# Delta rule's inverse: which engine splits the weights of the blocks beside it, and in which order the blocks run

## The chip, the cores and the metric

One NeuronCore of a Trainium2 chip runs the whole program. TensorE multiplies; VectorE, ScalarE and GpSimd do the rest; SyncE's queue (SP) issues nearly all DMAs. The metric is the device time of one execution in microseconds; the median of several runs counts. The granted TensorE clock has two levels here, 1.2 and 2.4 GHz, and the profile gives it as a share of full speed (1.00 is 2.4 GHz).

## The reference, cut to what matters

Two transformer blocks on 512 tokens of width 1024, in f32. The change is in the first block, whose first branch is a gated delta rule over 8 heads and two directions:

```python
a_kk = jnp.where(strict, jnp.einsum('bhnic,bhnjc->bhnij', kb, kc) * gam, 0.0)
sol = lax.linalg.triangular_solve(a_kk + eye, rhs, left_side=True, lower=True, unit_diagonal=True)
...                                     # a scan over the chunks makes o_a from sol
z = proj[..., C_ZA:C_AF].reshape(b, s, GDN_HEADS, GDN_HEAD_DIM)
o_a = _rmsnorm(o_a, norm_a[l]) * jax.nn.silu(z)
gate_a = jax.nn.sigmoid(proj[..., C_GA:C_GB])
gate_b = jax.nn.sigmoid(proj[..., C_GB:IN_COLS])
merged = (gate_a * jnp.einsum('bsc,cd->bsd', o_a, w_branch_a[l])
          + gate_b * jnp.einsum('bsc,cd->bsd', o_b, w_branch_b[l]))
```

Here `proj` is the normed input times `w_in`. The columns for z make 8 blocks of 128, and those for the two gates 16. Neither z nor the gates need the delta rule's result, so they can be worked out while the triangular inverse runs.

## The kernel before, in words

**A projection block.** An f32 product is made of three products of fp32r halves. `wload` (line 74 issues the load of 512 KB into `wraw`) lets ScalarE round the weights to `hi` (line 80) and another engine subtract to get `lo` (line 81), both in one tile `wpair`. `wraw` and `wpair` have three buffers each. `proj` then runs 8 x 3 products of 128 x 512 (lines 96 to 98) into one of the two banks named `pj`. Which engine subtracts is the argument `eng`; without it GpSimd takes the first three of the program and VectorE the others.

**The 24 blocks of this change** come from the generator `gates_z`. Every block ends with ScalarE's tanh out of `pj` into `gth` (line 697) and a store to DRAM (line 700, SP queue): z into `spill_z`, gates into `spill_g`. A z block (j below 8) has one step more: VectorE multiplies with `pj` again (line 699), so its bank of `pj` comes free only after that.

**Where they run.** `Fill` hands out blocks in the generator's order: 14 after the inverse of the 32 x 32 blocks has been issued, 1 inside the merge to 64, 4 inside the merge to 128, 3 in the tail of the delta rule, and 2 at the end of the dilated attention.

**The inverse.** `block_inverse` turns the layout through DRAM (scr), inverts 128 x 2 blocks of 32 x 32 on VectorE in a chain of 30 pairs of a product (line 498) and a sum (line 500), each dependent on the one before it, stores the result (line 503), loads it in another layout (`zd`, `zdT`, line 568) and transposes (lines 509 and 510). `merge32` then needs TensorE for many small products (lines 529, 540, 550), and `gdn_inverse` for those of 64 (lines 595, 604).

**What sets the order.** Each engine works through its own queue in order. The queues' order is made at build time by the framework's planner, which takes the program's order as priority and its own estimates of when an operand is ready; an operation that is ready earlier may be put ahead. A second inverse, in the second transformer block (`rwkv_inverse`, same lines 498 and 500, with `na_proj` and `gates2` beside it), is not touched; its blocks have their `lo` from VectorE.

Of the kernel before, what the change touches and what calls it, by code (L numbers as in the profile page):

```python
# [688 lines left out]
def gates_z(k, act, spill_z, spill_g):  # L689

    nc = k.nc
    for j in range(24):
        w = k.wload(k.a["w_in"][24 + j if j < 8 else 60 + j], eng=nc.gpsimd)
        ps = k.ps("pj")
        k.proj(ps, w, act)
        th = k.fp.tile([P, S], F32, name="gth", bufs=3)
        nc.scalar.activation(th, ps, AF.Tanh, scale=0.5)  # L697
        if j < 8:
            nc.vector.scalar_tensor_tensor(th, th, 1.0, ps, op0=OP.add, op1=OP.mult)  # L699
        nc.sync.dma_start(spill_z[j] if j < 8 else spill_g[j - 8], th)  # L700
        yield True
# [1133 lines left out]
def block1(k, a, pool, dram, tap, new_act, x_mid, x_1, acc_d, stop):  # L1835
# [10 lines left out]
    with pool("gkeep") as k.gk:  # L1846
        with pool("gprep") as k.gp:
            gdn_prep(k, act, R)
        tap("kT", R["kT"])
        fill = Fill(gates_z(k, act, spill_z, spill_g))  # L1850
        with pool("ginv") as k.ip:
            gdn_inverse(k, R, fill)
        tap("zt", R["zt"])
        with pool("gchain") as k.hp:
            gdn_chain(k, R)
        tap("oT", R["oT"])
# [240 lines left out]
```

## Time and profile before

| | |
|---|---|
| median of 3 runs | 2126.0 us (2125.77 to 2127.27) |
| the profiled execution | 2129.85 us, of it span 2128.2 us |
| TensorE products (PE) | 2013.3 us busy, 95% of the span |
| TensorE weight loads (PEld) | 1498.4 us, 70% |
| VectorE (DVE) | 1084.1 us, 51% |
| ScalarE (ACT) | 776.3 us, 36% |
| GpSimd (POOL) | 286.3 us, 13% |

The profile is of one execution, and times inside it are microseconds from the span's start. A busy share is a mean over stages with different limits, so the stage of the change, about 235 to 390 us, is read by itself below. In a timeline an entry in square brackets is the idle time of the engine before the instruction and what ended it; `x2` means two instructions merged into a row.

### The profile page before, as it was taken

Reading aid. Unit: us, or ns where it says so; the run is one execution under the profiler, and the core shown is the slowest. Engines: PE = TensorE matmul, PEld = TensorE weight load, DVE = VectorE, ACT = ScalarE, POOL = GpSimd, SP = SyncE. Lnnn points to the kernel's source line nnn. Section 1 sums busy time; section 2 is a strip of 40 time slices with the busy share of each in tenths; the row PEclk is TensorE's granted clock in tenths of the full one; section 3 lists DMA queues with packets and bytes.
Section 4 is the critical chain, followed back from the end, with each engine's and each line's share of the span. In section 5 each row is a group of like instructions: output and inputs, shape, how many; then the busy total and the mean of one; then the engine's idle time right before and its main releaser. Section 6 shows DMA issues by size and latency. Waiting matters only on the chain.

```text
span 2128.2 us, 30122 instructions
## 1 busy us (share of the span) xinstructions
PE 2013.3 (95%) x12072; PEld 1498.4 (70%) x12072; DVE 1084.1 (51%) x1877; ACT 776.3 (36%) x1357; POOL 286.3 (13%) x261
## 2 busy tenths in 40 slices
PE   6999987999999999999999999989899989799997
PEld 4777776977877787888888876666677778644443
DVE  6887492454234435632333266759337635435555
ACT  4556324432244333442233246645212622211111
POOL 1111342001000002110011001021123001110000
PEclk9999998999999999999999999989899999899999
DMA  4233535844221224422443533682674266499993
GB/s 153 109 129 119 159 135 129 261 147 143 94 73 66 70 80 160 164 91 99 166 142 109 168 108 97 180 231 78 177 249 144 85 227 242 140 421 425 423 423 159
DMA packets 161620, 360.46 MB, mean 169 GB/s; under 512 B 49592, under 2 KB 91192, under 8 KB 147136
## 3 DMA queue, kind: packets, MB, share of 16 engines
q1 hardware_dynamic: 153840, 321.49, 43.2%
q0 software_dynamic: 7200, 35.66, 4.9%
q8 instruction: 96, 1.57, 0.3%
q10 hardware_dynamic: 432, 1.31, 0.2%
q14 instruction: 52, 0.43, 0.1%
HBM read 300.74 MB, written 57.67 MB: 168 GB/s over the span
## 4 chain that ended last, share of the span: by engine, by line
PE 80%; DVE 9%; DMA 4%; issue 3%; POOL 2%; ACT 1%; SPq 1%; DVEq 0%; POOLq 0%; ACTq 0%
PE pj L97 15%; PE pj L98 15%; PE pj L96 15%; PE pj L1648 5%; PE pa L1677 2%; DVE x L500 2%; PE pa L98 2%; PE pa L96 2%; PE pa L97 2%; PE pb L97 1%; PE pb L98 1%; PE pb L96 1%; PE pb L1776 1%; PE pa L1776 1%; DVE xtmp L498 1%
## 5 line engine op out<-in xcount | busy, mean ns | idle before, releaser
L96 PE MATMUL pj<-hh,wpair 128*128 128x512 f32 (+1 forms) x1304 | 524.6, 403 | 8.7 <-DVE gth L699 5.6
L97 PE MATMUL pj<-hl,wpair 128*128 128x512 f32 (+1 forms) x1304 | 523.1, 401 | 1.0 <-DVE hl L151 1.0
L98 PE MATMUL pj<-hh,wpair 128*128 128x512 f32 (+1 forms) x1304 | 523.4, 402 | 0.5 <-issue 0.5
L81 DVE TENSOR_TENSOR wpair<-wraw,wpair 128x1024 fp32r<-128x1024 f32 x200 | 252.9, 1269 | 448.3 <-ACT wpair L80 448.2
L80 ACT CAST wpair<-wraw 128x1024 fp32r<-128x1024 f32 x227 | 236.4, 1046 | 196.1 <-PE pj L98 156.5
L96 PEld LDWEIGHTS pj<-hh,wpair 128*128 128x128 f32 x1304 | 251.9, 193 | 72.4 <-DVE gth L699 6.1
L98 PEld LDWEIGHTS pj<-hh,wpair 128*128 128x128 f32 x1304 | 251.6, 193 | 62.8 <-issue 9.3
L97 PEld LDWEIGHTS pj<-hl,wpair 128*128 128x128 f32 x1304 | 252.2, 193 | 60.3 <-issue 5.7
L1648 PE MATMUL pj<-wtwo,xgT 128*64 128x512 f32 x416 | 96.5, 603 | 0.0
L81 POOL TENSOR_TENSOR wpair<-wraw,wpair 128x1024 fp32r<-128x1024 f32 x27 | 65.8, 2443 | 159.7 <-ACT wpair L80 159.6
L378 DVE SCALAR_TENSOR_TENSOR cacc<-pj,convw,cacc 128x510 f32<-128x510 f32 (+1 forms) x96 | 71.3, 746 | 15.7 <-ACT cacc L374 14.4
L766 ACT COPY d<-pj 128x512 f32<-128x512 f32 x36 | 21.1, 587 | 133.8 <-PE pj L98 133.8
L1648 PEld LDWEIGHTS pj<-wtwo,xgT 128*64 128x64 f32 x416 | 28.4, 139 | 55.8 <-issue 53.1
L945 POOL TENSOR_TENSOR frelu<-frelu 128x512 f32<-128x512 f32 x32 | 33.4, 1042 | 232.1 <-ACT frelu L944 232.1
L944 ACT ACTIVATE frelu<-pj 128x512 f32<-128x512 f32 x32 | 19.2, 599 | 103.0 <-PE pj L98 103.0
L1677 PE MATMUL pa<-wtwo,ehT 128*64 128x512 f32 x208 | 50.0, 611 | 4.5 <-DMA wtwo<-in_w_dn 2.9
L1655 ACT ACTIVATE eth<-pj 128x256 f32<-128x256 f32 x16 | 6.1, 384 | 124.2 <-PE pj L1648 124.2
L500 DVE TENSOR_TENSOR x<-x,xtmp 128x60 f32<-128x60 f32 (+14 forms) x60 | 46.8, 780 | 1.6
L1778 DVE TENSOR_TENSOR x<-pa,x 128x512 f32<-128x512 f32 x64 | 43.2, 680 | 6.2 <-PE pa L1776 6.1
L1778 DVE TENSOR_TENSOR x<-pb,x 128x512 f32<-128x512 f32 x64 | 43.2, 680 | 5.7 <-PE pb L1776 5.7
L465 POOL TENSOR_TENSOR aq<-qT,egt 128x512 f32<-128x512 f32 x16 | 23.4, 1464 | 158.6 <-ACT egt L463 156.4
L697 ACT ACTIVATE gth<-pj 128x512 f32<-128x512 f32 x24 | 14.4, 599 | 82.3 <-PE pj L98 61.8
(603 smaller groups left out, 3529.4 us busy)
## 6 DMA issues: line engine op xcount, KB each, us to landing
wraw<-in_w_in SPq DMA_DIRECT2D x127, 512.0 KB, 3.3
wtwo<-in_w_gu SPq DMA_DIRECT2D x48, 1024.0 KB, 21.0
wraw<-in_w_ff SPq DMA_DIRECT2D x64, 512.0 KB, 3.3
wtwo<-in_w_dn SPq DMA_DIRECT2D x24, 1024.0 KB, 21.4
rld<-sp_rwkv POOLq DMA_DIRECT2D x16, 1024.0 KB, 5.4
wpair<-in_w_gu SPq DMA_DIRECT2D x12, 1024.0 KB, 22.0
spill_aq<-aq SPq DMA_DIRECT2D x16, 512.0 KB, 2.7
spill_g<-gth SPq DMA_DIRECT2D x32, 256.0 KB, 2.2
```

The source lines that it names most:

```text
L80: nc.scalar.copy(hi, raw)
L81: eng.tensor_sub(lo, raw, hi.bitcast(F32))
L96: mm(ps, lh, rh, start=start, stop=False)
L97: mm(ps, lh, rl, start=False, stop=False)
L98: mm(ps, ll, rh, start=False, stop=stop)
L378: nc.vector.scalar_tensor_tensor(acc[:, lo:hi], ps[:, lo + s:hi + s], cw[:, j:j + 1], acc[:, lo:hi], op0=OP.mult, op1=OP.add)
L500: nc.vector.tensor_add(x[:, :, 0:kk, kk + 1:32], x[:, :, 0:kk, kk + 1:32], t)
L945: nc.gpsimd.tensor_mul(r, r, r)
L1648: self.k.nc.tensor.matmul(self.ph[sl], self.x[:, 2 * b + c, sl], w[:, o, 512 * c:512 * c + 512], start=b + c == 0, stop=b + c == 4)
L1677: k.nc.tensor.matmul(self.po[h][sl], self.hT[:, c, sl], w[:, o, 512 * h:512 * h + 512], start=c == 0, stop=c == 1)
L1776: nc.tensor.matmul(ps, one[:, t * P:t * P + P], y[:, hs[h]], start=i == 0, stop=i == 1)
L1778: nc.vector.tensor_add(x, ps, x)
```

## The change

`gates_z` runs the same 24 blocks in another order (twelve gates, eight z, four gates), and lets VectorE instead of GpSimd do the subtraction of line 81 in all of them. Position by position: of the 14 blocks issued with the inverse, the first twelve are now gates and the last two are z; the merges have the next five z; the tail has the eighth z and two gates; the last two gates of all are as before.

```diff
 def gates_z(k, act, spill_z, spill_g):
 
     nc = k.nc
-    for j in range(24):
-        w = k.wload(k.a["w_in"][24 + j if j < 8 else 60 + j], eng=nc.gpsimd)
+    for j in (*range(8, 20), *range(8), *range(20, 24)):
+        w = k.wload(k.a["w_in"][24 + j if j < 8 else 60 + j], eng=nc.vector)
         ps = k.ps("pj")
         k.proj(ps, w, act)
```

## Rows read from the trace of the kernel before

**Rows 1.** The page: TensorE's busy tenths in 40 slices of the span.

```profile
PE   6999987999999999999999999989899989799997
```

**Rows 2.** TensorE's waits, 235 to 400 us: total us, times, longest.

```profile
PE pj L96 <- DVE gth L699: 5.6, 1, 5.6
PE pa L529 <- DVE zdT L509: 3.9, 1, 3.9
...
PE pa L529 <- issue: 1.8, 1, 1.8
PE pa L529 <- DMA zdT<-scr: 1.8, 1, 1.8
```

**Rows 3.** Timeline of VectorE, 225 to 400 us: start us, duration us.

```profile
260.81 0.19 DVE L498 TENSOR_TENSOR xtmp<-x 128x60 f32<-128x60 f32 x1
...
264.59 0.69 DVE L699 SCALAR_TENSOR_TENSOR gth<-gth,pj 128x512 f32<-128x512 f32 x1 [2.97 <-ACT gth L697]
...
265.87 2.42 DVE L500 TENSOR_TENSOR x<-x,xtmp 128x168 f32<-128x168 f32 x1
...
280.02 0.68 DVE L699 SCALAR_TENSOR_TENSOR gth<-gth,pj 128x512 f32<-128x512 f32 x1
...
312.67 0.33 DVE L500 TENSOR_TENSOR x<-x,xtmp 128x168 f32<-128x168 f32 x1
...
313.35 2.42 DVE L500 TENSOR_TENSOR x<-x,xtmp 128x116 f32<-128x116 f32 x1
...
316.06 0.22 DVE L500 TENSOR_TENSOR x<-x,xtmp 128x60 f32<-128x60 f32 x1
```

**Rows 4.** Timeline of GpSimd in the same stretch.

```profile
265.57 2.53 POOL L81 TENSOR_TENSOR wpair<-wraw,wpair 128x1024 fp32r<-128x1024 f32 x1 [8.80 <-ACT wpair L80]
270.61 5.34 POOL L81 TENSOR_TENSOR wpair<-wraw,wpair 128x1024 fp32r<-128x1024 f32 x2 [2.51 <-ACT wpair L80]
```

**Rows 5.** Timeline of ScalarE in the same stretch.

```profile
263.95 0.60 ACT L697 ACTIVATE gth<-pj 128x512 f32<-128x512 f32 x1 [5.00 <-PE pj L98]
264.45 1.04 ACT L80 CAST wpair<-wraw 128x1024 fp32r<-128x1024 f32 x1
...
300.37 0.60 ACT L697 ACTIVATE gth<-pj 128x512 f32<-128x512 f32 x1 [4.07 <-PE pj L98]
...
305.97 0.60 ACT L697 ACTIVATE gth<-pj 128x512 f32<-128x512 f32 x1 [4.07 <-PE pj L98]
```

**Rows 6.** Timeline of TensorE, at the stall and at the merge.

```profile
280.76 0.80 PE L96 MATMUL pj<-hh,wpair 128*128 128x512 f32 x1 [5.64 <-DVE gth L699]
...
328.64 2.25 PE L529 MATMUL pa<-zdT,zt 32*32 32x32 f32 x151 [1.75 <-DMA zdT<-scr]
```

**Rows 7.** Stretches: length, busy us by engine, granted clock (PEclk), DMA share, GB/s.

```profile
280.80:289.20 8.40, 8.40 (x25) 6.67 (x26) 8.02 (x14) 0.03 (x1) 0.00 (x0) 0.67 0.56 186
...
328.70:334.20 5.50, 3.68 (x252) 3.52 (x252) 4.29 (x4) 5.43 (x5) 0.00 (x0) 0.50 0.64 223
...
358.10:387.30 29.20, 29.20 (x346) 24.22 (x346) 5.50 (x8) 8.45 (x12) 9.56 (x4) 1.00 0.37 126
```

**Rows 8.** Timeline of the SP queue: DMA issues, start us, duration us.

```profile
316.31 0.80 SPq L503 DMA_DIRECT2D scr<-x  x2
317.20 0.73 SPq L700 DMA_DIRECT2D spill_g<-gth  x1
```

**Rows 9.** Timelines in the second inverse: VectorE, ScalarE, TensorE.

```profile
1442.38 1.22 DVE L81 TENSOR_TENSOR wpair<-wraw,wpair 128x1024 fp32r<-128x1024 f32 x1
...
1459.72 1.22 DVE L81 TENSOR_TENSOR wpair<-wraw,wpair 128x1024 fp32r<-128x1024 f32 x1
...
1452.30 1.04 ACT L80 CAST wpair<-wraw 128x1024 fp32r<-128x1024 f32 x1
...
1513.97 1.91 PE L529 MATMUL pa<-zdT,zr 32*32 32x32 f32 x198
...
1518.73 1.31 PE L540 MATMUL pa<-zd,yt 32*32 32x32 f32 x81
```

## The prediction

> **What bounds the kernel now.** I first read the forty slices of the page: TensorE is nearly full everywhere except at both ends and in the sixth and seventh slice (8 and 7 tenths), about 266 to 372 us [rows 1]. That is the delta rule's inverse, where the changed blocks run. Next the list of TensorE's waits from 235 to 400 us: 5.6 us for the z evacuation of line 699, then 3.9 us for VectorE's transpose and 1.8 us for the DMA of zdT, plus 1.8 us of issue [rows 2]. Nothing else there is over 3 us. So in this stretch TensorE is the bound, and it is held up in two places: once inside the blocks, once at the start of the merge.
>
> Then VectorE's timeline shows why. The inverse's chain (60 dependent operations, lines 498 and 500) runs from 260.81 to 316.28 us, 55.5 us [rows 3]. Nine of its operations are long: the first takes 2.42 us where one of the same size takes 0.33 us, the last 2.42 us [rows 3]. Each of the nine lies beside one of GpSimd's subtractions: the one at 265.87 beside 265.57 to 268.10, two more beside the pair from 270.61 [rows 4]. No chain operation away from them is long. The other thing in the chain is line 699: at 264.59 VectorE had stood idle for 2.97 us until ScalarE had the tanh [rows 3], since each engine works through its queue in order. And it hurts the other way round too: the sixth of these waits behind long chain operations until 280.02 [rows 3], the bank of pj stays occupied, and TensorE stands from 275.1 to 280.76, for 5.64 us [rows 6].
>
> **What a block costs.** Undisturbed blocks follow each other every 5.60 us (tanh at 300.37 and 305.97) [rows 5]. From 280.80 to 289.20, behind the stall, TensorE's granted clock averages 0.67 (part of it at 1.2 GHz, the rest at 2.4), and one block takes 8.40 us [rows 7].
>
> **Part 1: the chain without GpSimd beside it.** Chain now: 55.5 us. Blocked operations: 3 x about 2.1 = 6.2 beside the first three subtractions, and all nine add up to 18.2 us (1.6 to 2.1 each over the same size unblocked; first and last in [rows 3]). Idle before line 699: 3.0. Four evacuations inside the chain at 0.69: 2.8. Left: 55.5 - 18.2 - 3.0 - 2.8 = 31.5 us. With the change all 24 subtractions go to VectorE, at 1.22 us each, the price of line 81 between the chain operations of the second inverse [rows 9]. One comes per block, so some 7 fall within a chain of 40 us: 8.5 us. Chain: 31.5 + 8.5 = 40.0 us, so from 260.8 to 300.8. A wait is added here: each subtraction waits for ScalarE's hi, and behind it in VectorE's queue stand the chain's operations. The nearest row for that is the 2.97 us wait above; I take 1.2 us in all, bounds 0 and 4. End of chain: 302 (300.8 to 305).
>
> One rule of the Trainium skill speaks against this part. VectorE is busy for nearly the whole chain, and "Perfetto Trace Analysis", section "Optimizing Scalar/DVE Operations", says that with a saturated VectorE it may make sense to move work to ScalarE or even GpSimd; by that, 8.5 us are put back on the engine that is short. The same section warns that the two share a read port and the move might not help. The trace bears out the warning: a subtraction on GpSimd holds the chain up by some 2.0 us, more than the 1.22 us that it costs on VectorE itself. What the rule alone would make of the time is the last rival.
>
> **Part 2: gates first.** The twelve gate blocks need no VectorE: their bank is free after ScalarE's 0.60 us tanh [rows 5]. So the stall goes: 5.64 us. With it goes the low clock behind it: 8.40 - 5.60 = 2.80 us. TensorE would have its fourteen blocks done 8.4 us earlier than now, 322.7 - 8.4 = 314.3 instead of 322.7. The stores of the gates wait for ScalarE only, so the SP queue, whose weight loads stand behind them, gets on no later than now.
>
> What is late next: the weights. A pair made at the end of one block serves the third after it, so lo has 11.2 - 0.6 - 1.04 = 9.6 us from hi's end (tanh and cast, [rows 5]). The seventh load comes late: its cast begins at 264.45, ends at 265.5, and its block starts at 263.95 + 5.60 = 269.55 [rows 5]. There lo has 4.0 us, 2.8 beyond its own 1.22. With chain operations of at most 0.7 us ahead of it, this holds; I put it at 0 (the second rival is what happens if not).
>
> **Part 3: the merge.** The data for its second half reach TensorE at 328.64 [rows 6], 12.4 us after the chain's end, through two stores [rows 8], two loads and a transpose. With the chain's end at 302 they come at 314.4. Two weight loads and a store of a gate will now run beside these transfers, so 0 to 3 us more; I take 1.3: 315.7. TensorE is ready at 314.3 + 0.5 (part 4), so it waits 1 to 1.5 us instead of 3.90 + 1.75 = 5.65 [rows 2, 6]: gain 4.15, bounds 0 (chain at 305, 3 us more) and 5.65. The first part of the merge took 5.6 us at a clock of 0.50 (328.70 to 334.20) [rows 6, 7]. In the second inverse, where TensorE comes to it out of full blocks, the same 256 products took 4.8 us (1513.97 to 1518.73) [rows 9]. Gain 0.8; the upper bound is 2.75, half of the 5.5 us.
>
> The order in the queues supports this. The SP queue holds the chain's stores (316.31) ahead of a gate's store issued at 317.20, though that gate's tanh ran at 305.97 [rows 5, 8]. So the planner, which sets the order of each engine's queue, reckoned with the chain's end before the end of the block whose tanh that is; without TensorE's loss of 8.4 us that block ends at 297.6. So its reckoning has no blocked operations in it, and a chain without them runs about as ordered.
>
> **Part 4: what it costs.** (a) Three subtractions fall into the preparation, where VectorE is busier: the last may delay the final zt by one price, 0 to 1.22; I take 0.5. (b) The z blocks now lie beside the merge: from 358.10 to 387.30 VectorE is busy 5.50 of 29.20 us [rows 7]; four subtractions and four evacuations add 4 x 1.91 = 7.6, and each block of 5.6 us covers its 1.9. In order they can hold up a yt or zt copy by 1.9 at most; I take 0.5 in all, bounds 0 and 2. If the cover is gone, each such round costs up to 1.9. (c) The last two subtractions come in the dilated stage, 0 to 2.4; I take 0. (d) The eighth z goes to DRAM with the twentieth block, long before the tail's loads: 0. The order of the other four gates is as it was: 0.
>
> **The sum.** 5.64 + 2.80 + 4.15 + 0.8 - 0.5 - 0.5 = 12.4 us. The profiled execution took 2129.85 us (span 2128.2 and 1.65 around it): 2117.5 by this. It lies 3.85 us above the median of the runs, so against the median: 2126.0 - 12.4 = 2113.6 us. A measurement of this kernel can tell some 0.2% (4.3 us) from no change.
>
> **Rivals.**
> *The merge stays the bound.* TensorE saves its 8.4 us in the blocks, but the chain ends at 305 or later (in-order waits on hi) and the transfers take their 3 us more: arrival at 320.4, a wait of 5.6 again and the same low clock. For it: the 2.97 us wait, and the transfers' share of the path. Against it: no subtraction in the second inverse cost the chain such a wait. Gain 8.4 - 1 = 7.4: 2118.6 us.
> *Late weights.* In the second inverse one subtraction began at 1459.72, though its hi was done at 1453.34: 6.4 us behind [rows 9]. If this falls on the seventh or eighth load, where 2.8 us are spare, TensorE waits 3.6 us and gets the lower clock for another 2.8: 6.4 us per event, and two of them undo the gain. For it: that row. Against: the others there came 0 to 3 us behind, with no such wait on TensorE. Time: 2120 with one, 2126 with two. The change not doing what it says is close to this: the planner treats the new order as a wish and pulls z blocks into the chain, the stall stays, and of the sum only parts 3 and 4 remain, 4.0 us: 2122.
> *VectorE serves the chain first (slower).* The chain is emitted ahead of the blocks. If its operations go first, subtractions wait for the chain's end. The seventh block, due at 269.55, then starts at about 260.8 + 31.5 + 1.2 = 293.5; eight of the fourteen are left (5.60 each), 44.8 us: the merge begins at 338.3 instead of 328.64, and the wait leaves 2.8 of low clock: 9.7 to 12.5 us slower, some 2137 us. It decides from the point where a subtraction lies more than 9.6 us behind its hi. Against it: eight subtractions lie between the chain operations of the second inverse [rows 9].
> *The saturated engine.* If the long operations aren't GpSimd's doing, they stay: chain 55.5 - 3.0 - 2.8 + 8.5 = 58.2 us, end 319, arrival 331.4 instead of 328.64: 2.7 us later, and with part 4's bounds 5 us: 2129 to 2131. It is the rule quoted in part 1 taken alone. Nine of nine beside GpSimd speaks against it.
>
> **Chances.** Forecast 0.60 (2108.5 to 2118); merge the bound 0.17 (2118 to 2121.5); late weights or z pulled in 0.12 (2120 to 2129); chain first 0.08; saturated engine 0.03. The best case is 5.64 + 2.80 + 5.65 + 2.75 with no costs, 16.8, some 2109; the upper end takes in the merge rival with part 4's costs (1 + 1.2 + 2.4 more, in part): 2124. The range 2108.5 to 2124 leaves out about 0.2. Faster by over 0.2% (below 2121.7): 0.60 + 0.16 = 0.76; within: 0.13; slower: 0.11.
>
> **What would show it.** Right: no chain operation over 0.7 us; chain from about 260 to 302; no wait of TensorE on line 699 between 260 and 315; clock 1.00 through the fourteen blocks; the first merge products near 315; everything from the first 64-wide products (358.07) on some 12 us earlier. Wrong: waits of TensorE on line 81; a chain of over 48 us; waits on line 699 or on yt between the merge's products; or a later stage that gives back the 12 us, for which I have no row.

## The result, and the profile after

The changed kernel takes 2102.5 us (median, 2097.7 to 2111.1), the kernel before 2125.9 beside it: ratio 0.9882, 95% interval 0.9851 to 0.9913, so 18 to 32 us faster. I had forecast 12.4 us, and 2108.5 to 2124.0. The direction held, the size didn't: the gain is some 20 us. Two more takes of the same kernel beside their own runs of before give 0.9900 and 0.9915 (both below), which is 21 and 18 us: more, each time, than the 16.8 us of my best case.

The profiled executions are 18.7 us apart (2129.85 and 2111.12 us). What answers to [rows 1], TensorE's slices on the page of after, has 9 and 8 in the sixth and seventh slice, where before had 8 and 7. The 8 that is left holds the merge:

```profile
PE   6999998999999999999999999989899989799997
```

TensorE's waits from 205 to 400 us (total us, times, longest) answer to [rows 2]. The 5.6 us on line 699 are gone, and of 5.65 us at the start of the merge 0.5 is left. What stays is issue (time in which the profile shows nothing that the engine waited for) at the merge's later products:

```profile
PE pa L540 <- issue: 3.3, 2, 2.5
PE pa L550 <- issue: 2.5, 1, 2.5
PE pa L529 <- DVE zdT L509: 0.5, 1, 0.5
PE pb L444 <- DVE vT L382: 0.2, 1, 0.2
```

VectorE's timeline answers to [rows 3]. Its chain has no operation over 0.7 us any more; the subtractions of line 81 stand between its operations at 1.22 us each. It runs from 251.17 to 297.52 us and once waits 3.35 us for ScalarE's rounding:

```profile
251.17 0.20 DVE L498 TENSOR_TENSOR xtmp<-x 128x60 f32<-128x60 f32 x1
...
255.35 0.47 DVE L500 TENSOR_TENSOR x<-x,xtmp 128x300 f32<-128x300 f32 x1
259.17 1.22 DVE L81 TENSOR_TENSOR wpair<-wraw,wpair 128x1024 fp32r<-128x1024 f32 x1 [3.35 <-ACT wpair L80]
260.32 0.50 DVE L498 TENSOR_TENSOR xtmp<-x 128x336 f32<-128x336 f32 x1
...
297.30 0.22 DVE L500 TENSOR_TENSOR x<-x,xtmp 128x60 f32<-128x60 f32 x1
```

TensorE's timeline at the merge answers to [rows 6]. Half of the 256 products of line 529 need VectorE's transpose of the first load (line 509), the other half the second load. In before the first of them started at 326.64, after a wait for the transpose, and then waited again, for the load:

```profile
326.64 0.25 PE L529 MATMUL pa<-zdT,zt 32*32 32x32 f32 x4 [3.90 <-DVE zdT L509]
```

In after they start at 309.81, and products of the next projection block run between the first eight of them and the other 248, where the wait used to be:

```profile
309.81 0.31 PE L529 MATMUL pa<-zdT,zt 32*32 32x32 f32 x8 [0.47 <-DVE zdT L509]
310.06 0.50 PE L97 MATMUL pj<-hl,wpair 128*128 128x512 f32 x1
...
312.12 2.31 PE L529 MATMUL pa<-zdT,zt 32*32 32x32 f32 x248
```

Stretches of after (length, busy us of PE, PEld, DVE, ACT, POOL, granted clock, DMA share, GB/s) answer to [rows 7]: full clock through all of the fourteen blocks, the low level (0.50) only in a later part of the merge, and full again in the 64-wide products:

```profile
232.20:307.70 75.50, 75.50 (x327) 61.25 (x327) 48.69 (x81) 21.10 (x30) 2.63 (x2) 1.00 0.68 200
...
322.90:328.20 5.30, 2.76 (x144) 2.63 (x132) 1.37 (x2) 1.94 (x4) 0.00 (x0) 0.50 0.11 40
...
336.30:365.50 29.20, 29.20 (x346) 24.04 (x345) 12.07 (x16) 8.46 (x12) 0.00 (x0) 1.00 0.35 122
```

**Where the time went.** I set the same instruction of both traces side by side. The first tanh of the changed blocks (ScalarE, before, then after):

```profile
241.55 0.60 ACT L697 ACTIVATE gth<-pj 128x512 f32<-128x512 f32 x1 [0.94 <-PE pj L98]
```

```profile
235.25 0.60 ACT L697 ACTIVATE gth<-pj 128x512 f32<-128x512 f32 x1 [1.63 <-PE pj L98]
```

and the first 64-wide product (TensorE, before, then after):

```profile
358.07 0.74 PE L595 MATMUL pa<-zT,zt 64*64 64x64 f32 x18
```

```profile
336.25 0.86 PE L595 MATMUL pa<-zT,zt 64*64 64x64 f32 x22
```

At the first 64-wide product after is 21.8 us ahead. Of these, 1.1 lie between the starts of the programs and the transposition of kT at 207.18 (206.08 after), which come and go (205.5 to 208.2 over all the traces below, with no regard to the edit). The rest, by stage:

| stage | before | after | saved | forecast |
|---|---|---|---|---|
| preparation: transposition of kT to first tanh | 34.4 | 29.2 | 5.2 | -0.5 |
| the fourteen blocks: first tanh to the end of the 14th | 81.15 | 72.45 | 8.7 | 8.44 |
| merge to 64: from there to the first product of line 595 | 35.4 | 28.55 | 6.85 | 4.95 |
| 64-wide products, z blocks beside them (to line 644) | 29.2 | 29.2 | 0 | -0.5 |
| from line 644 to the end | 1740.9 | 1743.9 | -3.0 | 0 |

The preparation is the surprise: I had put a small cost there. Of the 3 us at the end, 2.5 lie in the second block, between line 975 and the copy of line 491, a stretch that takes 168.7 to 174.1 us over all traces (169.0 in before, 171.5 in after; more on it at the last experiment). They don't return in the other two traces of the changed kernel (1737.1 and 1740.1 to the end).

### The profile page after: what moved, and what is told of

The parts are those of the page before. It is cut to its first block, busy times and chain, and to the rows that moved or that the text cites. A ratio compares the mean times of both kernels' runs of the same rounds, so it can differ in the third digit from the quotient of the medians.

```text
span 2109.4 us, 30119 instructions
## 1 busy us (share of the span) xinstructions
PE 2004.9 (95%) x12072; PEld 1492.4 (71%) x12072; DVE 1091.3 (52%) x1901; ACT 775.9 (37%) x1357; POOL 227.7 (11%) x237
## 4 chain that ended last, share of the span: by engine, by line
PE 81%; DVE 7%; issue 4%; DMA 3%; POOL 2%; ACT 2%; SPq 0%; DVEq 0%; POOLq 0%; ACTq 0%
PE pj L97 15%; PE pj L96 15%; PE pj L98 15%; PE pj L1648 5%; PE pa L1677 2%; PE pa L98 2%; PE pa L96 2%; PE pa L97 2%; PE pb L97 1%; PE pb L98 1%; PE pb L96 1%; PE pb L1776 1%; PE pa L1776 1%; DMA wtwo<-in_w_dn 1%; PE pb L821 1%
## 5 line engine op out<-in xcount | busy, mean ns | idle before, releaser
L81 DVE TENSOR_TENSOR wpair<-wraw,wpair 128x1024 fp32r<-128x1024 f32 x224 | 282.3, 1264 | 475.7 <-ACT wpair L80 473.0
L80 ACT CAST wpair<-wraw 128x1024 fp32r<-128x1024 f32 x227 | 236.3, 1045 | 198.9 <-PE pj L98 161.5
L1770 DVE SCALAR_TENSOR_TENSOR yl<-pa,wslot,yh 128x512 fp32r<-128x512 f32 x32 | 24.0, 751 | 36.7 <-ACT yh L1769 35.0
L1091 PE MATMUL pa<-rar,rkb 64*128 64x128 f32 x256 | 31.1, 311 | 7.4 <-DVE rmu L1096 7.0
## 6 DMA issues: line engine op xcount, KB each, us to landing
wpair<-in_w_gu SPq DMA_DIRECT2D x12, 1024.0 KB, 21.8
```

The lines of the kernel that those rows point to most:

```text
L80: nc.scalar.copy(hi, raw)
L81: eng.tensor_sub(lo, raw, hi.bitcast(F32))
L1091: nc.tensor.matmul(pg[:, x], row(e, cc), ar[H[e], cc].rearrange("p s x -> p (s x)"), start=True, stop=True)
```

## The experiments

The theory behind them: the long chain operations and the preparation's extra 5 us both come from GpSimd's subtractions, which hold VectorE up, and the order of the blocks does the rest. The rivals: the order alone does it; the 5 us in the preparation are chance, since single executions differ by as much; and not GpSimd's reading but its being at work, or the order of the queues, makes VectorE slow.

All ratios are against the kernel before, run beside on the same chip, with 95% intervals. "Stage" is from the first tanh (line 697) to the first product of line 595 in the profiled execution.

| kernel | median, us | ratio | first tanh | stage |
|---|---|---|---|---|
| before | 2125.9 to 2130.4 in five sets | 1 | 241.6 | 116.5 |
| after | 2102.5 | 0.9882 [0.9851, 0.9913] | 235.3 | 101.0 |
| after, second take | 2106.5 | 0.9900 [0.9867, 0.9932] | 235.7 | 101.6 |
| after, third take | 2111.6 | 0.9915 [0.9888, 0.9942] | 235.0 | 100.7 |
| order only | 2121.8 | 0.9962 [0.9938, 0.9985] | 237.1 | 111.1 |
| engine only | 2110.4 | 0.9912 [0.9887, 0.9937] | 235.9 | 104.5 |
| before, first three on VectorE | 2120.1 | 0.9972 [0.9950, 0.9994] | 236.1 | 114.9 |
| after, first three on GpSimd | 2107.1 | 0.9893 [0.9870, 0.9917] | 242.6 | 100.5 |
| both subtract | 2137.0 | 1.0038 [1.0010, 1.0066] | 243.5 | 118.1 |
| GpSimd writes only | 2107.2 | 0.9898 [0.9837, 0.9958] | 234.8 | 100.5 |
| fourteen gates | 2108.7 | 0.9909 [0.9884, 0.9934] | 235.7 | 101.3 |
| dxr on VectorE | 2101.1 | 0.9864 [0.9829, 0.9899] | 236.3 | 101.6 |
| dxr on VectorE, second take | 2101.5 | 0.9881 [0.9854, 0.9907] | 235.9 | 99.3 |
| dxr on VectorE, first three on GpSimd | 2103.8 | 0.9895 [0.9867, 0.9923] | 240.9 | 100.3 |

**The two halves of the change.** The new order, the subtractions still on GpSimd:

```diff
-        w = k.wload(k.a["w_in"][24 + j if j < 8 else 60 + j], eng=nc.vector)
+        w = k.wload(k.a["w_in"][24 + j if j < 8 else 60 + j], eng=nc.gpsimd)
```

> The new order of blocks alone; the subtraction stays on GpSimd. Theory A (three separate parts: GpSimd's subtraction delays VectorE in the preparation, about 5 us with the low clock behind it; VectorE's z evacuations inside the chain stall TensorE, 8.4 us; GpSimd's subtractions lengthen the chain and so delay the merge, about 7 us): only the second part goes, and the merge then waits for the chain, which still has its long operations: chain 55.5 - 3.0 - 2.8 = 49.7 us, end near 309, data at the merge near 322 instead of 328.6. First tanh of the blocks at 241 to 242 us as before, operations of 2 us and more still in the chain, 5 to 7 us faster than before. Theory B (the order is what counts, and the shift of 6 us in the preparation is chance): 15 us or more faster.

And VectorE with the old order:

```diff
-    for j in (*range(8, 20), *range(8), *range(20, 24)):
+    for j in range(24):
```

> The subtraction on VectorE, blocks in the old order (z first). Theory A: the preparation's 5 us and the chain's blocked operations go: first tanh near 236 us, no chain operation over 0.8 us, and the evacuations of z, now behind short operations, no longer come 9 us late, so most of the 8.4 us of the stall goes too: 14 to 19 us faster than before. Theory B: the bank stall of z first stays, 8 us of TensorE's time, and VectorE's queue is only fuller: 0 to 8 us faster.

The order alone is 8 us faster (3 to 13), the engine alone 19 (13 to 24). One expectation missed: with the order alone the first tanh came at 237.1 us, not at 241 to 242, and the merge's data with it at 317 instead of 322 (why, see the first three blocks). The waits of TensorE say where the two gains come from. Order only, 205 to 400 us: no wait on line 699, but the merge waits longer than before, 7.1 us instead of 5.65, since nine operations of the chain are still long (2.5 to 2.9 us) and TensorE is there earlier:

```profile
PE pa L529 <- DVE zdT L509: 5.5, 1, 5.5
...
PE pb L444 <- DVE vT L382: 2.5, 2, 2.1
...
PE pa L529 <- DMA zdT<-scr: 1.6, 1, 1.6
```

Engine only: no wait on line 699 either, although the z blocks still run beside the chain, and little at the merge:

```profile
PE pa L529 <- issue: 1.5, 1, 1.5
PE pa L529 <- DVE zdT L509: 1.0, 1, 1.0
```

So the stall of 5.64 us needed both z blocks and long chain operations; either edit removes it. By stage the engine is worth 12.0 us with the old order and 10.1 with the new one, the order 5.4 with GpSimd and 3.5 with VectorE. Together they give 15.5 us and not 17.4: both remove the stall, and the order alone hands part of it back in the longer wait at the merge. By time the order's part on top of the engine's isn't clear of noise (18 to 25 us for both in three takes, 19 for the engine alone).

**The first three blocks.** Their subtractions fall into the preparation. On VectorE in the kernel before, and on GpSimd in the changed one:

```diff
-        w = k.wload(k.a["w_in"][24 + j if j < 8 else 60 + j], eng=nc.gpsimd)
+        w = k.wload(k.a["w_in"][24 + j if j < 8 else 60 + j], eng=nc.vector if j < 3 else nc.gpsimd)
```

> Old order, and GpSimd keeps the subtraction except for the first three blocks, whose weights are made in the preparation (205 to 235 us). Theory A: TensorE's wait of 2.1 us for line 382's vT near 215 us and the low clock from 215 to 225 us go; first tanh near 236.5 instead of 241.5, everything after it as before: about 5 us faster. Theory B (the 5 us in the preparation are chance, or come from elsewhere): first tanh at 241, no faster than before.

```diff
-    for j in (*range(8, 20), *range(8), *range(20, 24)):
-        w = k.wload(k.a["w_in"][24 + j if j < 8 else 60 + j], eng=nc.vector)
+    for i, j in enumerate((*range(8, 20), *range(8), *range(20, 24))):
+        w = k.wload(k.a["w_in"][24 + j if j < 8 else 60 + j], eng=nc.gpsimd if i < 3 else nc.vector)
```

> New order, VectorE subtracts except for the first three blocks, which GpSimd keeps. Theory A: the wait for vT near 215 us and the low clock behind it are back, first tanh near 240 to 241 us, the chain and the merge are as in the changed kernel: about 5 us slower than the changed kernel, 13 to 18 us faster than before. Theory B: as fast as the changed kernel, 19 to 23 us faster than before.

In the traces the three subtractions decide the preparation's length. From the transposition of kT to the first tanh it is 29.1 to 29.2 us in all nine traces in which VectorE alone makes them, in either order, and 34.4 (before), 34.4 and 34.4 (the two kernels with the three back on GpSimd; the second is the last experiment) and 31.4 (order only) with GpSimd. So it isn't chance. What follows keeps its length within 1.6 us (stage 114.9 against 116.5, and 100.5 against 101.0). The row that I missed stands in the trace of before, a little ahead of where I began to read. TensorE from 206 to 216 us:

```profile
207.18 0.60 PE L444 MATMUL pb<-ident,kT 128*128 128x128 f32 x4
...
214.85 1.09 PE L444 MATMUL pb<-ident,vT 128*128 128x128 f32 x4 [2.12 <-DVE vT L382]
```

GpSimd and VectorE in the same stretch of before:

```profile
210.09 2.40 POOL L81 TENSOR_TENSOR wpair<-wraw,wpair 128x1024 fp32r<-128x1024 f32 x1 [10.34 <-ACT wpair L80]
212.45 1.71 POOL L465 TENSOR_TENSOR aq<-qT,egt 128x512 f32<-128x512 f32 x1
```

```profile
211.12 1.91 DVE L172 TENSOR_TENSOR edec<-egt,edec 128x512 fp32r<-128x512 f32 x1
212.96 1.75 DVE L382 SCALAR_TENSOR_TENSOR vT<-cth,cacc 128x512 f32<-128x512 f32 x1
```

`edec` is long beside GpSimd's subtraction, and `vT` beside a product that stood behind that subtraction in GpSimd's queue. Unhindered they take 0.68 and 0.67 us, so the two holds are 2.3 us. My estimate from these rows: without them `vT` would have been done 5.2 us after the transposition of kT began (7.53 - 2.3), and TensorE came for it at 5.55 (214.85 - 2.12 - 207.18), so there would have been no wait. TensorE, VectorE and GpSimd in after:

```profile
206.08 0.60 PE L444 MATMUL pb<-ident,kT 128*128 128x128 f32 x4
...
214.58 0.66 PE L444 MATMUL pb<-ident,vT 128*128 128x128 f32 x4 [0.23 <-DVE vT L382]
```

```profile
209.24 1.22 DVE L81 TENSOR_TENSOR wpair<-wraw,wpair 128x1024 fp32r<-128x1024 f32 x1
210.37 1.78 DVE L172 TENSOR_TENSOR edec<-egt,edec 128x512 fp32r<-128x512 f32 x1
...
213.85 0.67 DVE L382 SCALAR_TENSOR_TENSOR vT<-cth,cacc 128x512 f32<-128x512 f32 x1
```

```profile
210.06 1.55 POOL L465 TENSOR_TENSOR aq<-qT,egt 128x512 f32<-128x512 f32 x1 [11.41 <-ACT egt L463]
```

`edec` is long here too, beside that same product, which now runs earlier; `vT` isn't.

From the transposition of kT, `vT` is done 7.53 us later in before (212.96 + 1.75 - 207.18) and 8.44 later in after. So its data come 0.9 us *later* with the subtraction on VectorE, within what I had allowed for. The wait is gone because TensorE's queue has another order. Between the two transpositions stand 8 projection products in before and 15 in after, and also the pair of lines 181 and 182 and one product of line 467; over all twelve traces with these lines the count goes with the engine of the first three: 8 in the four with GpSimd, each with a wait of 2.11 or 2.12 us, and 15 in the eight with VectorE, each with one of 0.23 or 0.24. I read it so: the subtraction on VectorE is time that the planner reckons with, so it put `vT` late and filled in; that an operation on GpSimd holds VectorE's up isn't in its reckoning, so there it put the transposition too early, and TensorE stood. The orders and the holds are shown, the planner's reason is inferred.

Behind the wait the granted clock may fall to its lower level for a while. Stretch 213 to 225 us, before, then after, then order only:

```profile
213.00:225.00 12.00, 10.15 (x34) 7.54 (x35) 5.87 (x13) 3.95 (x9) 2.43 (x2) 0.72 0.46 175
```

```profile
213.00:225.00 12.00, 11.77 (x61) 9.41 (x62) 9.09 (x18) 6.11 (x13) 1.61 (x1) 1.00 0.46 177
```

```profile
213.00:225.00 12.00, 11.64 (x54) 9.02 (x55) 7.32 (x16) 5.16 (x10) 3.69 (x2) 1.00 0.44 168
```

Order only has the same wait of 2.11 us and keeps its clock. So the wait costs the preparation 2.2 us (31.4 against 29.2), and 5.2 with the low clock behind it (34.4), which came in three of the four traces that have the wait.

By time the term is harder to see. In the old order it is 6.0 us (1.3 to 10.6). In the new one the median speaks for theory B: 22 us faster than before, where theory A said 13 to 18, and no difference between 2107.1 and the 2106.5 us of the second take, which ran on another chip and whose interval is as wide as the term. So it was tried again on a kernel with less spread (the last experiment).

**What about GpSimd holds VectorE up?** First GpSimd subtracts as before, and then VectorE does it over again:

```diff
+            nc.gpsimd.tensor_sub(lo, raw, hi.bitcast(F32))
```

> The changed kernel, in which GpSimd makes each subtraction of the 24 blocks first and VectorE then makes it again: the suspected cost is added and nothing else taken away. Theory A (a chain operation that meets a GpSimd subtraction waits until it is done): again some 8 operations of 2 us and more in the chain, chain near 46.4 + 8 x 2.0 = 62 us instead of 46.4, zd later by as much, TensorE waits at the merge for 8 us or more, 8 to 14 us slower than the changed kernel. Theory B (long operations come from something else, such as the z evacuations or the transfers): chain at 46 to 49 us, as fast as the changed kernel.

Then GpSimd only fills the same tile, twice per block, before VectorE subtracts:

```diff
+            for _ in range(2):
+                nc.gpsimd.memset(lo.bitcast(F32), 0.0)
```

> The changed kernel, in which GpSimd fills lo with zeros twice, ahead of VectorE's subtraction, in each of the 24 blocks: GpSimd is busy beside the chain, but reads nothing. Theory A in its narrow form (what holds VectorE is GpSimd's reading beside an operation with two operands in SBUF): no chain operation over 0.8 us, chain 46 to 48 us, time as the changed kernel. Theory A in its wide form (any GpSimd operation holds VectorE): some 8 to 16 operations longer by about 1 us, chain 55 to 60 us.

With both subtracting, the long operations are back (VectorE, then GpSimd; lines are shifted by 2). VectorE's own subtraction is held up as well, 3.42 us for 1.22:

```profile
272.16 2.66 DVE L500 TENSOR_TENSOR xtmp<-x 128x396 f32<-128x396 f32 x1
274.74 3.42 DVE L83 TENSOR_TENSOR wpair<-wraw,wpair 128x1024 fp32r<-128x1024 f32 x1
```

```profile
271.85 5.22 POOL L82 TENSOR_TENSOR wpair<-wraw,wpair 128x1024 fp32r<-128x1024 f32 x2 [2.02 <-ACT wpair L80]
```

The chain takes 63.0 us, as expected (62), with seven long operations. The kernel is 8 us slower than before (2 to 14) and 31 slower than the second take of after, where I had expected 8 to 14. I had left out that the subtractions now wait for GpSimd too: TensorE waits for weights (6.7 us in four waits), 5.5 us for `vT` in the preparation, and 8.0 us at the merge. With GpSimd only writing, it is busy for somewhat less long (1.96 us a block against 2.3 to 2.8 in before), nine times beside the chain, and no operation of the chain is over 0.7 us (GpSimd, then a chain operation within its pair of fills; lines are shifted by 3):

```profile
279.41 1.97 POOL L82 MEMSET wpair<- 128x1024 f32 x2 [3.61 <-PE pj L101]
```

```profile
279.95 0.65 DVE L503 TENSOR_TENSOR x<-x,xtmp 128x476 f32<-128x476 f32 x1
```

Its time (two runs) and stage are those of the changed kernel. So it isn't GpSimd at work that costs, nor its writing: what the subtraction does and the fill doesn't is read. (One tile read or two, that was not separated.) On VectorE's side it takes an operation that reads two tiles from SBUF. In before line 699, which reads one tile from SBUF and the other, `pj`, from PSUM, ran wholly beside a subtraction and took its usual 0.68 us; the chain operation behind it was held (VectorE, then GpSimd):

```profile
290.99 0.68 DVE L699 SCALAR_TENSOR_TENSOR gth<-gth,pj 128x512 f32<-128x512 f32 x1
291.59 2.25 DVE L498 TENSOR_TENSOR xtmp<-x 128x476 f32<-128x476 f32 x1
```

```profile
290.79 2.54 POOL L81 TENSOR_TENSOR wpair<-wraw,wpair 128x1024 fp32r<-128x1024 f32 x1 [11.69 <-ACT wpair L80]
```

The Trainium skill has this rule in "SBUF — State Buffer", section "Who interferes with whom": a VectorE instruction with two SBUF inputs contends with a GpSimd instruction that reads SBUF, and not with one that only writes there. The runs agree, with some 2.0 us of hold per subtraction on the one side and none on the other.

**Do the last two z blocks beside the chain cost anything?** Fourteen gates first:

```diff
-    for j in (*range(8, 20), *range(8), *range(20, 24)):
+    for j in (*range(8, 22), *range(8), *range(22, 24)):
```

> The changed kernel with fourteen gates first, then the eight z, then two gates: no evacuation of z on VectorE between the chain's end and the transposes (302.85 and 309.59 us in the changed kernel), three z blocks in the delta rule's scan instead of one. Theory A (without GpSimd's subtractions the place of the z blocks matters little): within 3 us of the changed kernel. Theory B (the place of z matters by itself): 3 us or more to either side, shown by a wait of TensorE on line 699 or by transposes that come earlier than 10.9 us after the chain's end.

2108.7 us and a stage of 101.3: no difference from after (2106.5 beside it, stage 100.7 to 101.6). After's two z blocks come when the chain is done.

**How far apart are executions of one kernel?** The changed kernel twice more:

> The changed kernel once more, for its time beside the two half changes and for a second trace. Theory A: first tanh of the blocks at 235 to 236 us, chain of 46 to 47 us, no wait of TensorE for vT over 0.5 us in the preparation, first 64-wide products 100 to 102 us after the first tanh (116.5 before, 104.5 with the engine alone, 111.1 with the order alone); time 18 to 26 us below before, where the spread comes from the granted clock in the dilated stage (540 to 860 us), which neither part touches: 438.8 us from the tail's first product to the feed-forward stage in the traces with low clocks there, 429 to 433 without. Theory B (the change itself moves the dilated stage): that stretch is always 429 to 433 here.

> The changed kernel once more, beside the next one, so that both have the same runs of the kernel before. If the gain of the change is as its two earlier takes, 2106 to 2112 us in the profiled run and a median between 2102 and 2109 us. From the first tanh (L697) to the first row product of the next stage (L595) 101 to 102 us, as in the two traces of it so far. From the dilated stage's first store of scores (L715) to the first product on L944, a stretch the change doesn't touch, the traces so far gave 434.1 and 438.8 us; if what lies between is chance, this one may be anywhere from 428 to 442.

The stage is 100.7 to 101.6 us in all three. The median of the third take, 2111.6, lies above the 2102 to 2109 that I had expected. The spread (2097.7 to 2122.3 over 24 runs) lies elsewhere. Much of it is in the dilated stage, from line 715 to line 944, which the change doesn't touch but for its last two blocks: it takes 438.8, 434.1 and 432.6 us, and 428.8 to 441.8 in order only, engine only and the two first-three kernels. TensorE waits there four times for `dxr`, a pair of products that GpSimd and VectorE share. In the third take one such wait has a low clock behind it, products at 0.63 instead of 0.39 us:

```profile
579.29 0.39 PE L96 MATMUL pj<-hh,wpair 128*128 128x512 f32 x1
580.89 0.58 PE L853 MATMUL pa<-dxr,ones 8*128 8x512 f32 x1 [1.21 <-POOL dxr L848]
...
582.00 0.63 PE L98 MATMUL pj<-hh,wpair 128*128 128x512 f32 x1
```

So the same remedy was tried there, all of `dxr` on VectorE (the edit of line 848; line 851 likewise):

```diff
-                (nc.vector if h else nc.gpsimd).tensor_mul(xr.rearrange("k (m r) -> k m r", r=4), row[:, :, None].to_broadcast([8, P, 4]),
+                nc.vector.tensor_mul(xr.rearrange("k (m r) -> k m r", r=4), row[:, :, None].to_broadcast([8, P, 4]),
```

> The changed kernel, and in the dilated stage the first half of each pair of products into dxr (L848, L851) on VectorE instead of GpSimd, as the second half already is. In the trace of the changed kernel TensorE waits for this tile 3.9 us in four waits of up to 1.2, each pair of products takes 1.04 and 2.26 us on GpSimd and 1.32 and 2.19 on VectorE at the same time, and the clock behind these waits is 0.96 in 540 to 780 us in one execution and 0.98 to 1.00 in another. Theory one (each of these waits can set off a low clock, and the spread of the executions comes from that): the four waits shrink to 2 us or less in sum, the stretch from L715 to L944 takes 426 to 429 us, and the median falls by 2 to 10 us against the changed kernel, with less spread. Rival (the low clock comes by itself, or VectorE alone takes as long for both halves as the two engines beside each other): the waits stay at 3 to 5 us or the stretch stays at 432 to 442, and the median is within 2 us of the changed kernel.

The tile's operations (duration min/median/max in ns), in the third take of after and in this kernel:

```profile
L848 POOL TENSOR_TENSOR dxr<-dlt,sel x4: 1383/2262/2271, 578.6 to 775.4; 8x512 fp32r<-8x512 f32 x4
L848 DVE TENSOR_TENSOR dxr<-dlt,sel x4: 1778/2188/2196, 579.5 to 775.9; 8x512 fp32r<-8x512 f32 x4
```

```profile
L848 DVE TENSOR_TENSOR dxr<-dlt,sel x8: 1035/1051/1062, 582.1 to 774.0; 8x512 fp32r<-8x512 f32 x8
```

Two beside each other take 2.2 us, and one after the other on VectorE 2 x 1.05: sharing them gained nothing. The waits are gone, 540 to 780 us now runs full:

```profile
540.00:780.00 240.00, 235.89 (x1140) 188.18 (x1139) 97.33 (x152) 98.54 (x186) 16.21 (x11) 0.99 0.22 75
```

```profile
540.00:780.00 240.00, 240.00 (x1164) 191.36 (x1163) 97.10 (x160) 99.62 (x188) 5.17 (x4) 1.00 0.24 80
```

The dilated stage takes 427.3 us, the median is 2101.1 against 2111.6 of the third take beside it, and the six runs lie within 9 us, where the third take's twelve lie within 22. That is theory one, with a fall of 10.5 us, just above the 2 to 10 expected. The second take gave 2101.5. These are the lowest medians here, though the first take of after (2102.5) isn't clear of them.

**The first three blocks once more, on this steadier kernel.** The kernel with `dxr` on VectorE again, and the same with the first three subtractions on GpSimd (the edit is the one above):

> The kernel with dxr on VectorE once more, as the partner of the next one, since its runs lie closer together (2097 to 2106 us) than those of the changed kernel (2100 to 2122). Expected: a median between 2098 and 2105 us, the stretch from L715 to L944 427 to 429 us, no wait for dxr; first tanh near 236 us.

> The kernel before this one, with the subtractions of the first three blocks back on GpSimd, so that the term of the preparation stands alone in two kernels whose late stages are steadier. If the trace's reading holds (GpSimd's subtraction beside vT and the others holds VectorE up, TensorE waits 2.1 us for vT on L444 and its clock may fall behind it), this one is slower by 2 us (the wait alone) to 7 us (with the low clock behind it): first tanh 239 to 243 us against 236, a median of 2103 to 2109. If the preparation's term is nothing, as the two medians with and without it in the changed kernel had it (2107.1 against 2106.5), both medians are within 1.5 us of each other though the wait on L444 is there.

2101.5 against 2103.8 us: 2.3 us slower, in the expected range but at its lower end (the intervals of their ratios overlap). The trace has the wait of 2.12 us on line 444, a clock of 0.72 behind it and a preparation of 34.4 us instead of 29.2, so 5.2 us, and it is 6.7 us behind at line 944. In these two executions all of it is given back, 5.4 between line 975 and the copy of line 491 in the second block, where this one takes 168.7 us and its partner 174.1. There both wait alike for TensorE's operands on line 1091 (7.0 and 6.8 us in six waits), but the clock behind these waits was 0.94 and 0.72 in 1340 to 1380 us here, and 0.83, 0.53 and 0.87 in 1333.5 to 1393.5 in the partner. So what was given back comes from the clock in a stage that the edit doesn't touch, and not from the edit. How much of the preparation's 5 us the medians keep is open between some 2 us and all of it, since the low clock behind the wait need not come in each execution.

## Why the prediction was wrong in size

**What bounds (right).** Both of the places named gave way, and by the mechanism named: no chain operation over 0.7 us, no wait on line 699, clock 1.00 through the fourteen blocks.

**Part 1 (mechanism right, length and start off).** The chain takes 46.35 us, not 41.2: eight subtractions instead of seven, and 5.6 us of in-order waits for ScalarE's rounding (3.35, 1.63, 0.34, 0.30) where I took 1.2 and bounded by 4. It ends at 297.5, not 302, and outside my bounds of 300.8 to 305; that it came no further off is luck, since a chain 5.1 us too short was set against a start 9.6 us too late. It starts at 251.17: 6.3 us come from what lies before the first tanh, and 3.3 because the copy into `x`, whose data had landed at 256.4 us (issued at 251.18, 5.2 to landing), stood behind a z block's line 699 in VectorE's queue (timeline of before):

```profile
258.99 0.69 DVE L699 SCALAR_TENSOR_TENSOR gth<-gth,pj 128x512 f32<-128x512 f32 x1 [4.91 <-ACT gth L697]
259.59 1.11 DVE L491 COPY x<-xraw 128x1024 f32<-128x1024 f32 x1
```

I had removed the evacuations inside the chain and not the one ahead of it.

**Part 2 (right).** 8.44 forecast, 8.7 measured. But I gave the gain to the order alone; either edit brings it.

**Part 3 (right in kind, 1.9 us too small).** The transfers did get slower, by about the 1.3 us that I took: the second load landed 12.3 us after the chain's end in before, and 13.7 and 13.8 us after it in the second and third take (in after itself no wait shows its landing). The first products start 12.3 us after the chain's end, in before 10.4. But TensorE doesn't stand until the second load is there, since projection products run in between: the wait is 0.47 us. I had left 1.5 in the sum, though my own terms (315.7 - 314.8) leave 0.9. That is 1.0 of the 1.9. The rest is at the merge's products: while projection products run among the first of them the clock is 1.00 (308 to 316 us), and the low clock comes only in a later part (0.50 in 322.9 to 328.2). That these products hold the clock up is my reading; no run takes them away.

**Part 4 (a): the step that failed.** "The last may delay the final zt by one price, 0 to 1.22; I take 0.5", a cost that excluded a gain. Measured: a preparation shorter by 5.2 us, 5.7 us off my term. Of the 5.2, some 2.2 are the wait and its holds, and 3.0 the low clock behind it, which order only shows need not come. Two things were wrong. My list of waits began at 235 us, while the first of the 24 subtractions ran at 210, so a wait of 2.12 us that the removed operation caused was never read. And I priced the operation where it goes and not what it had cost where it was. The traces of the experiments on the first three blocks pin the term to them in both orders; the times show it in the old order (1.3 to 10.6 us), and in the new one not clear of noise.

**Part 4 (b, c) (cost too high).** The 64-wide products take 29.2 us as before, with the z blocks beside them.

**The sum.** 5.2 + 8.7 + 6.85 + 0 = 20.75 us against 12.4. Of the 8.35 between, 5.7 is Part 4 (a), 1.9 Part 3, 0.5 Part 4 (b) and 0.25 Part 2. My best case, 16.8, held no gain in the preparation, and that is the main reason why the range missed. The 23.4 us between the medians are 2.7 more than the stages give; the three takes of after lie 18.8 to 23.4 below their runs of before, so that much is within the spread of executions.

**The rivals.** None came. The chain exceeded neither 48 us nor did a later stage give the gain back. The saturated engine is refuted by VectorE itself: it has more to do (1091.3 us busy in the whole execution against 1084.1), and yet the long operations are gone and its chain is shorter by 9 us.

## What to carry to other kernels

When an operation leaves an engine, list the waits of every stretch in which it ran, from its first instance on, before pricing where it goes: three of 24 brought a quarter of what this pair of traces gained by the first 64-wide product. Beside a chain of operations that read two tiles, a subtraction on GpSimd cost VectorE more (2.0 us) than doing it itself (1.22 us). Such a hold can show at a third engine, as a wait: here TensorE's, which cost up to 5.2 us. Two edits that remove the same stall don't add in full.

## What the runs showed of the hardware

I had not expected that a wait of TensorE of one to two microseconds costs so differently from one execution to the next: behind the 2.1 us on line 444 the clock in 213 to 225 us was 0.72 in three traces (before and the two with the first three back on GpSimd) and 1.00 in a fourth, order only; behind the waits of up to 1.2 us on `dxr` the mean clock of 540 to 780 us was 0.96 in before and in after, 0.99 in the second and third take and 1.00 in order only. Without the waits on `dxr` the runs of a kernel lie closer together: their standard deviation is 2.3 to 3.7 us in three sets of six, and 4.2 to 7.3 in the sets of four runs and more with them. So such small waits seem to make much of the spread here; that they do is argued from these numbers and not shown run by run.
